# Moving where the low weight halves and the rows of x begin in SBUF, in a one-layer hybrid decoder step

## The chip, the core and the metric

The kernel runs as one program on one core of a Trainium2 chip. The metric is the device time of one execution in microseconds, the median of several runs. The profiled execution is a run of its own: its span is the time from its first to its last recorded instruction, and it has its own device time beside that.

## The reference, cut to what matters

One decoder layer works on 304 tokens: 16 meta tokens, a prompt of 256, and 8 samples of 4 tokens. Nearly all arithmetic is matrix products with float32 weights:

```python
D_MODEL = 2048; D_FF = 5632
def decoder_layer(x, ...):
    xn = rms_norm(x, norm_mix)
    z = xn @ w_in                     # 7456 columns, split between two mixers
    o_a, S_a = rwkv7_mixer(z_a, ...)  # 16 heads of 64, a recurrence over the tokens
    o_b, S_b = retention_mixer(z_b, ...)  # 4 heads of 256, in chunks
    h = x + concatenate([o_a, o_b]) @ w_out
    hn = rms_norm(h, norm_ffn)
    h = h + (silu(hn @ w_gate) * (hn @ w_up)) @ w_down
```

A final norm follows, and the states of both mixers are returned for prompt and samples. The meta tokens are needed by the mixers only: the outputs of the layer have 288 tokens.

## The kernel before, in words

**Tiling.** Features lie on the 128 partitions and tokens run along the free dimension, so a row of x is one feature group `k` (16 of them) with 304 tokens per partition. A weight matrix is cut into blocks of 128 x 128. Four blocks make a tile of 512 columns, which one DMA brings into `wr` in the order of their use.

**Three products for one.** float32 accuracy comes from splitting each operand into two `float32r` halves. ScalarE writes the high half `wh` of a weight tile (a CAST), VectorE the low half `wl = wr - wh`. x is split in the same way into `xh` and `xl`. Each weight block then takes three TensorE matmuls into one accumulator: `wh` with `xh`, `wh` with `xl`, `wl` with `xh` (lines 751 to 753, the three `self.pe.matmul` of `main`). Each has its own weight load, which the profile lists under PEld; it runs beside the matmul before it. All vector, scalar and tensor instructions of the program are listed under line 318, the helper that records them.

**Stages.** First come the 59 blocks of columns of the input projection ("the mixed stages" here), with the mixers' own small matmuls, vector and scalar work between them. The accumulators take 304 columns, 290 (the r columns and two of the loras) or 288 (the retention's q and gates), starting at token 0, 14 or 16 of the row. Then the output projection overwrites the rows `xh` and `xl` with the mixers' outputs, 288 columns of them, and after it with the input of the FFN. The FFN runs gate and up blocks on those rows, and down blocks on activations which lie in the arena `arena_dt.float32r`, also 288 columns.

**Order.** A planner with a cost table decides at build time which step comes next, and the order is then kept on every engine. A first pass (a draft) also measures how long each scratch tile lives; `Room.place` packs them into two arenas, whose limit is `ROOM`.

**Addresses.** Tiles of the pools get SBUF addresses in the order in which the pools were opened (lows, const, weights, scratch) and the tiles made. A row of `xh` is padded from 304 to `XW` = 320 elements, 1280 bytes, so that all rows begin at the same place modulo 256 bytes. `self.xh` is the view for the mixed stages, `self.xf` the one for the stages behind, shifted by `SHIFT_X` elements. The activations of the FFN are shifted by `SHIFT_A` in the same way. These are the begins in the compiled program, in bytes modulo 256:

| what | before | after |
|---|---|---|
| `wl`, all 5 buffers | 128 | 96 |
| `wh`, all 5 buffers; `wr` | 64 | 64 |
| rows of x, mixed stages, 304 columns | 128 | 144 |
| the same from token 14 (290 columns) | 184 | 200 |
| the same from token 16 (288 columns) | 192 | 208 |
| rows of x behind the mixed stages | 208 | 208 |
| FFN activations in the arena | 208 | 208 |
| `sums` (weights of the small sums) | 224 | 224 |

Of the kernel before, what the change touches and what calls it, by code (L numbers as in the profile page):

```python
# [9 lines left out]
F32R = mybir.dt.float32r  # L10
# [5 lines left out]
P = 128  # L16
D = 2048
KT = D // P
# [4 lines left out]
T = META + SEQ + NB * NS  # L23
# [51 lines left out]
NCV = _o  # L75


SHIFT_X = [20] * KT
SHIFT_A = [20] * 11


LASTK = T - P
KEYS = ((0, META, SEQ, 0), (P, P, NP - P, SEQ), (LASTK, 2 * P, T - 2 * P, SEQ + NP - P))
RMW = SEQ + NP - P + T - 2 * P
ROOM = 33008
WIDE = 3792
FREE, GAPS, TRIES = 800.0, (2000.0, 1000.0, 500.0, 200.0, 50.0, 0.0), 12

# [519 lines left out]
class Step:  # L608
# [213 lines left out]
    def start(self):  # L822
        I = self.I
        self.pvt = self.t([P, NPV], "pv", pool=self.cp)
        self.ones = self.t([P, P], "ones", pool=self.cp)
        self.dve.memset(self.ones, 1.0)

        self.omu = self.t([P, 46], "omu", pool=self.cp)
        self.eps = {}
        for c, e in enumerate((RMS_EPS, GN_EPS, 4 * RMS_EPS), 27):  # L830
            self.eps[e] = self.omu[:, c:c + 1]
            self.pool.memset(self.eps[e], e)
        xh, xl = self.xh, self.xl
        warm = self.t([P, 1], "warm")
        self.act.activation(warm, self.ones[:, :1], AF.Tanh)

        gx = self.t([P, KT + KT * T], "xr")
        self.gx = gx[:, :KT]
        xr = self.xr = gx[:, KT:].rearrange("p (k t) -> p k t", t=T)
        x = lambda a, b: self.sp.dma_start(xr[:, a:b], xT(I)[:, a:b, :])  # L840
        self.sp.dma_start(gx[:, :KT + T], I["xT"][:, :KT + T])
        self.load(2)
        x(1, 2)
        self.load(2)
        self.sp.dma_start(self.pvt, I["pv"])
        x(2, 3)
        self.load(2)
        x(3, 4)
        self.load(2)
        for k in range(4, KT, 2):  # L850
            self.load()
            x(k, k + 2)
        self.converted = 0

        pt = self.ps(WARM)
        for _ in range(WARM):
            self.pe.matmul(pt[:, :P], self.ones, self.ones, start=True, stop=True)
# [1074 lines left out]
    def build(self, gam4):  # L1932
        self.gam4 = gam4
        self.shifts = 0
        self.os, self.on, self.gates, self.ht, self.xs_of = [None] * KT, {}, {}, [], {}
        xh = self.t([P, KT, XW], "xh", F32R, pool=self.cp)
        xl = self.t([P, KT, XW], "xl", F32R, pool=self.cp)
        self.xh, self.xl = xh[:, :, :T], xl[:, :, :T]
        self.xf = [(xh[:, k, s:s + TO], xl[:, k, s:s + TO]) for k, s in enumerate(SHIFT_X)]
        self.xs = [(self.xh[:, k, :], self.xl[:, k, :]) for k in range(KT)]  # L1940
        jobs = [self.z_job(i, self.lora_post(i), c0=META - 2 if i else 0) for i in range(3)]
        for h in range(NPAIR):
            jobs += self.pair_jobs(h)
        for h in range(RH):
            jobs += self.ret_jobs(h) + self.gate_jobs(h)
        jobs += self.out_jobs(0) + self.out_jobs(1) + self.ffn_jobs()
        jobs = {j.key: j for j in jobs}
        self.raws, self.halves, self.rests, self.loaded, self.halved = [], [], [], 0, 0
        self.start()
        self.plan.run(self.main(jobs))  # L1950
        self.flush(all=True)
# [5 lines left out]
def xT(I):  # L1957

    return I["xT"][:, KT:].rearrange("p (k t) -> p k t", t=T)
# [19 lines left out]
def body(tc, I, O):  # L1979
# [6 lines left out]
    rooms[F32R].place(WIDE)  # L1986
    rooms[F32].place(ROOM - rooms[F32R].size)
    with ExitStack() as ctx:
# [23 lines left out]
```

## Time and profile before

| | us |
|---|---|
| median of 3 runs (1532.53 to 1534.03) | 1532.96 |
| the profiled execution: device time | 1533.73 |
| its span | 1532.0 |
| PE (matmuls) busy | 1516.4 |
| DVE (VectorE) busy | 1087.0 |
| ACT (ScalarE) busy | 883.7 |

A matmul's record lasts longer than the distance to the next matmul, since they are pipelined. What a matmul costs when TensorE is never idle is therefore read from starts: the length of an unbroken stretch over the number of matmuls in it. The chain of waits lists such stretches with a start, a length and a count. "acc" are the large products of `main`, "mm" the small ones of the mixers.

### The profile page before, as it was taken

What the parts mean: (1) busy time and instruction counts of PE and PEld (TensorE: products, weight loads), DVE (VectorE), ACT (ScalarE), POOL (GpSimd) and SP (SyncE); (2) the same over time, 40 slices, a digit from 0 to 9 for tenths busy, and PEclk for the clock granted to TensorE, in tenths of its full rate; (3) what the DMA queues carried; (4) which work ended last, traced back from release to release, by engine and by line L of the source; (5) the groups of instructions that cost most, each with busy time, mean ns of one, the idle gap of its engine ahead of it and who ended that gap; (6) DMA issues with size and microseconds to landing.
All of it is one profiled execution on the core that took longest, in us unless ns stands there. A gap on an engine that the chain in (4) does not pass through costs nothing.

```text
span 1532.0 us, 31962 instructions
## 1 busy us (share of the span) xinstructions
PE 1516.4 (99%) x11428; PEld 1498.7 (98%) x11428; DVE 1087.0 (71%) x2769; ACT 883.7 (58%) x2109; POOL 32.1 (2%) x165
## 2 busy tenths in 40 slices
PE   8999999999999999999999999999999999999997
PEld 8999999999999989999999999999999999999997
DVE  6989997999999688776656565656565656565656
ACT  6786779878866875577444444444444444444445
POOL 0010010000000000000000000000000000000000
PEclk9999999999999999999999999999999999999999
DMA  7545543544444369756655555555555555555554
GB/s 234 178 138 158 168 144 115 171 151 148 135 138 132 117 241 320 224 177 212 187 158 172 159 169 162 169 162 166 164 164 165 165 163 167 166 163 165 166 166 131
DMA packets 138927, 258.57 MB, mean 169 GB/s; under 512 B 16272, under 2 KB 22928, under 8 KB 138768
## 3 DMA queue, kind: packets, MB, share of 16 engines
q1 hardware_dynamic: 138768, 256.52, 53.6%
q8 instruction: 91, 1.49, 0.4%
q14 instruction: 68, 0.56, 0.1%
HBM read 242.18 MB, written 14.28 MB: 167 GB/s over the span
## 4 chain that ended last, share of the span: by engine, by line
PE 92%; DVE 3%; ACT 2%; DMA 1%; issue 1%; SPq 0%; DVEq 0%; POOL 0%; ACTq 0%
PE acc L318 82%; PE mm L318 10%; DVE arena_dt.float L318 1%; ACT arena_dt.float L318 1%; DMA wr<-big 1%; DVE wl L318 1%; ACT wh L318 0%; ACT xh L318 0%; DMA arena_dt.float<-xT 0%; DVE xl L318 0%; SPq L318 0%; DVE arena_dt.float32r L318 0%; ACT arena_dt.float32r L318 0%; DVEq L2008 0%; POOL arena_dt.float L318 0%
## 5 line engine op out<-in xcount | busy, mean ns | idle before, releaser
L318 PE MATMUL acc<-xh,wh 128*128 128x288 f32 (+2 forms) x2592 | 787.3, 304 | 2.0 <-ACT wh L318 2.0
L318 PE MATMUL acc<-xh,wl 128*128 128x288 f32 (+2 forms) x2592 | 770.3, 297 | 0.6 <-DVE wl L318 0.6
L318 PE MATMUL acc<-xl,wh 128*128 128x288 f32 (+2 forms) x2592 | 764.2, 295 | 0.0
L318 ACT CAST wh<-wr 128x512 fp32r<-128x512 f32 (+1 forms) x827 | 503.5, 616 | 370.1 <-PE acc L318 322.9
L318 DVE TENSOR_TENSOR wl<-wr,wh 128x512 fp32r<-128x512 f32 (+1 forms) x827 | 561.5, 685 | 128.8 <-ACT wh L318 126.4
L318 PEld LDWEIGHTS acc<-xh,wh 128*128 128x128 f32 x2592 | 487.8, 188 | 6.3 <-issue 2.7
L318 PEld LDWEIGHTS acc<-xl,wh 128*128 128x128 f32 x2592 | 487.8, 188 | 3.0 <-issue 1.9
L318 PEld LDWEIGHTS acc<-xh,wl 128*128 128x128 f32 x2592 | 484.3, 187 | 1.7 <-DVE wl L318 1.4
L318 PE MATMUL acc<-arena_dt.float32r,wh 128*128 128x288 f32 x1408 | 281.5, 295 | 0.2 <-DVE arena_dt.float L318 0.2
L318 PEld LDWEIGHTS acc<-arena_dt.float32r,wh 128*128 128x128 f32 x1408 | 226.7, 189 | 0.6 <-DVE arena_dt.float L318 0.4
L318 PE MATMUL acc<-arena_dt.float32r,wl 128*128 128x288 f32 x704 | 208.8, 297 | 0.0
L318 DVE TENSOR_TENSOR arena_dt.float<-acc,arena_dt.float 128x288 f32<-128x288 f32 (+4 forms) x181 | 72.6, 419 | 156.9 <-PE acc L318 156.3
L318 DVE TENSOR_TENSOR arena_dt.float<-arena_dt.float 128x288 f32<-128x288 f32 (+21 forms) x658 | 159.7, 279 | 8.6 <-ACT arena_dt.float L318 6.3
L318 PE MATMUL mm<-arena_dt.float 128*128 128x128 f32 (+7 forms) x1120 | 161.9, 299 | 2.0 <-ACT arena_dt.float L318 1.2
L318 DVE TENSOR_TENSOR arena_dt.float<-arena_dt.float,acc 128x288 f32<-128x288 f32 (+1 forms) x210 | 94.2, 450 | 95.4 <-PE acc L318 93.9
L318 ACT ACTIVATE arena_dt.float<-arena_dt.float 128x288 f32<-128x288 f32 (+7 forms) x229 | 97.1, 432 | 103.1 <-DVE arena_dt.float L318 101.5
L318 PEld LDWEIGHTS mm<-arena_dt.float 128*128 128x128 f32 (+1 forms) x1120 | 138.4, 181 | 8.2 <-ACT arena_dt.float L318 1.9
L318 PEld LDWEIGHTS acc<-arena_dt.float32r,wl 128*128 128x128 f32 x704 | 131.7, 187 | 0.0
L318 ACT COPY arena_dt.float<-mm 64x64 f32<-64x64 f32 (+11 forms) x338 | 94.9, 289 | 45.0 <-PE mm L318 40.8
L318 ACT COPY arena_dt.float<-arena_dt.float 128x8 f32<-128x8 f32 (+8 forms) x267 | 62.5, 283 | 26.6 <-DVE arena_dt.float L318 25.3
L318 ACT CAST arena_dt.float32r<-arena_dt.float 128x288 fp32r<-128x288 f32 (+6 forms) x117 | 49.7, 429 | 40.5 <-DVE arena_dt.float L318 40.1
L318 DVE TENSOR_TENSOR arena_dt.float32r<-arena_dt.float,arena_dt.float32r 128x288 fp32r<-128x288 f32 (+6 forms) x116 | 52.1, 451 | 18.3 <-ACT arena_dt.float32r L318 18.0
(68 smaller groups left out, 571.7 us busy)
## 6 DMA issues: line engine op xcount, KB each, us to landing
wr<-big SPq DMA_DIRECT2D x823, 256.0 KB, 2.7
arena_dt.float<-s0r SPq DMA_DIRECT2D x24, 512.0 KB, 6.4
out_rts<-arena_dt.float SPq DMA_DIRECT2D x16, 512.0 KB, 4.3
arena_dt.float<-s0w SPq DMA_DIRECT2D x16, 256.0 KB, 3.2
arena_dt.float<-xT SPq DMA_DIRECT2D x4, 576.0 KB, 6.3
arena_dt.float<-lora SPq DMA_DIRECT2D x16, 128.0 KB, 2.7
out_rws<-arena_dt.float SPq DMA_DIRECT2D x8, 256.0 KB, 3.4
arena_dt.float<-xT SPq DMA_DIRECT2D x6, 304.0 KB, 5.8
```

The costliest lines, as they stand in the source:

```text
L318: return self._plan.keep(f(*a, **k))
```

## The change

An unused tile `gap` of 56 elements (224 bytes) is made first in the pool of the lows, so that all tiles behind it lie 224 bytes further on; `omu` in the pool of constants grows by 8 elements (32 bytes), so that the tiles behind that one lie 256 bytes further on and begin where they did modulo 256. The view of x for the mixed stages begins 12 elements into the padded row, and the shift behind them grows from 20 to 28. The limit of the arenas is lowered by 64 elements, to pay for the 256 bytes. The arenas come out with the sizes they had, and every engine issues the same instructions in the same order as before.

```diff
-SHIFT_X = [20] * KT
+FIRST = 12
+SHIFT_X = [28] * KT
 SHIFT_A = [20] * 11
...
-ROOM = 33008
+ROOM = 32944
...
-        self.omu = self.t([P, 46], "omu", pool=self.cp)
+        self.omu = self.t([P, 54], "omu", pool=self.cp)
...
+        gap = self.t([P, 56], "gap", F32R, pool=self.lp)
         xh = self.t([P, KT, XW], "xh", F32R, pool=self.cp)
         xl = self.t([P, KT, XW], "xl", F32R, pool=self.cp)
-        self.xh, self.xl = xh[:, :, :T], xl[:, :, :T]
+        self.xh, self.xl = xh[:, :, FIRST:FIRST + T], xl[:, :, FIRST:FIRST + T]
         self.xf = [(xh[:, k, s:s + TO], xl[:, k, s:s + TO]) for k, s in enumerate(SHIFT_X)]
```

## The prediction

> **What bounds the kernel now.** I read the busy shares first, then the waits of PE, then busy time by stretch.
>
> ```profile
> PE 1516.4 (99%) x11428; PEld 1498.7 (98%) x11428; DVE 1087.0 (71%) x2769; ACT 883.7 (58%) x2109; POOL 32.1 (2%) x165
> ```
>
> ```profile
> PE acc L318 <- ACT wh L318: 2.0, 2, 1.7
> PE acc L318 <- DVE wl L318: 0.6, 3, 0.3
> ```
>
> ```profile
> 400.00:500.00 100.00, 100.00 (x783) 99.88 (x782) 94.20 (x397) 69.56 (x206) 6.11 (x30) 1.00 0.43 132
> 730.00:1490.00 760.00, 760.00 (x5703) 760.00 (x5702) 441.42 (x793) 321.16 (x555) 0.00 (x0) 1.00 0.54 166
> ```
>
> In the last two rows the columns are PE, PEld, DVE, ACT and POOL busy, the granted clock, the DMA share and GB/s. PE waits for weight halves for under 3 us in all. In the FFN (730 to 1490) it is busy without a gap at full granted clock, while DVE is busy for 58% and ACT for 42% of the time. In the mixed stages PE has no gap either, but DVE stands at 94%. So the time is a sum of matmul pitches, from one start to the next, and the question is what sets a pitch. The chain of waits (start, length, what, count) gives it:
>
> ```profile
> 607.24 56.48 PE acc L318 x438
> 687.31 5.44 PE acc L318 x42
> 695.31 4.40 PE acc L318 x33
> 702.28 5.06 PE acc L318 x39
> 709.91 4.80 PE acc L318 x36
> 717.28 4.28 PE acc L318 x33
> 722.41 772.22 PE acc L318 x5790
> 1495.16 21.94 PE acc L318 x168
> ```
>
> All of these are 288-column matmuls on data at 208 modulo 256. Yet the first row has 56.48 / 438 = 128.95 ns each, the seventh 772.22 / 5790 = 133.37 ns, and the short ones between them 129.5, 133.3, 129.7, 133.3 and 129.7. Operands, engine and clock are the same, and the pitch has two values. Single starts show that it isn't a mixture:
>
> ```profile
> 645.24 0.29 PE L318 MATMUL acc<-xh,wl 128*128 128x288 f32 x1
> 645.37 0.29 PE L318 MATMUL acc<-xh,wh 128*128 128x288 f32 x1
> 645.50 0.29 PE L318 MATMUL acc<-xl,wh 128*128 128x288 f32 x1
> 645.63 0.29 PE L318 MATMUL acc<-xh,wl 128*128 128x288 f32 x1
> ...
> 845.32 0.30 PE L318 MATMUL acc<-xh,wl 128*128 128x288 f32 x1
> 845.45 0.30 PE L318 MATMUL acc<-xh,wh 128*128 128x288 f32 x1
> 845.58 0.29 PE L318 MATMUL acc<-xl,wh 128*128 128x288 f32 x1
> 845.72 0.30 PE L318 MATMUL acc<-xh,wl 128*128 128x288 f32 x1
> ```
>
> Three matmuls take 0.39 us in the first piece (645.24 to 645.63) and 0.40 us in the second. Each state repeats itself once it is entered; a stop of the stream (the small matmuls between the short stretches) lets it be entered anew. I read this as PE's own reads of SBUF meeting each other: the columns of one matmul are read while the weights of the next are loaded (PEld busy 760.00 of 760.00 us), and where they meet hangs on both addresses and on the phase in which the stream started. DVE and ACT start and stop all through the FFN without breaking the rhythm, so they are not the cause. The FFN fell into the long rhythm at 722.41 and had no stop until 1494.63.
>
> **The change part by part.** *Work.* No instruction is added, removed or moved: all five engines have the same sequence, the arenas the same sizes and places within. `gap` is never written. So every term is a change of duration.
>
> *Writes of VectorE and ScalarE at the new places.* `wl` is now written at 96 and, in the first 40 us, x at 144.
>
> ```profile
> L318 DVE TENSOR_TENSOR wl<-wr,wh 128x512 fp32r<-128x512 f32 x823 | 559.9, 686 | 127.8 <-ACT wh L318 125.4 <-PE acc L318 1.3
> L318 DVE TENSOR_TENSOR xl<-arena_dt.float,xh 128x288 fp32r<-128x288 f32 x16 | 6.8, 453 | 1.9 <-ACT xh L318 1.9
> L318 ACT ACTIVATE xh<-arena_dt.float 128x304 fp32r<-128x304 f32 x16 | 8.3, 544 | 4.0 <-DMA arena_dt.float<-xT 4.0
> L318 ACT ACTIVATE xh<-arena_dt.float,pv 128x288 fp32r<-128x288 f32 x16 | 7.8, 530 | 9.9 <-DVE arena_dt.float L318 9.9
> ```
>
> The second row writes at 208, 16 bytes off a multiple of 64, the first at 128, on it: (686 - 453) / (512 - 288) = 1.04 ns an element, and 288 x 1.04 + 153 = 453, with 686 - 512 x 1.04 = 153, puts both on a plain line through a usual fixed part. ScalarE: 544 - 530 = 14 ns for 16 more elements, on 128 and 208. I take nothing for these writes. The cover is thin in the mixed stages alone: 10 ns more on each of their some 240 `wl` subtractions would be 2.4 us on DVE at 94%, and at most that on the path.
>
> *FFN: `wl` from 128 to 96.* x and activations stay at 208, `wh` at 64, so of the three weight loads one meets other addresses, and the lows begin in the middle of a 64-byte piece. The only row with weights at such a begin is the small sums (`sums`, 224), too short for a rhythm. Bounds: the short rhythm that the same stage has shown, (133.37 - 128.95) x 5790 = **-25.6 us**; a longer one. For the latter I need a step. The rhythms seen are, for three matmuls of 288 columns, 3 x 128.95 = 386.9, 3 x 133.37 = 400.1, and, with x at 192 in the mixed stages, this one:
>
> ```profile
> 390.69 5.51 PE acc L318 x42
> 452.45 12.80 PE acc L318 x96
> ```
>
> 5.51 / 42 = 131.2 ns, 393.6 for three; the other is 133.3 again. The steps are some 6.6 ns a triple, 2.2 ns a matmul. One step longer would be 2.2 x 5790 = +12.7 us, two +25.5 us; I take one as the bound. Of the two sides I take the short rhythm: the pitch of 133.4 is the longest that an unbroken stretch of 288 columns shows here, and two thirds of its meetings keep their places, so a new third has more ways to break it than to lengthen it. But this is a judgment and not a row: of five short stretches with everything at the old places three were short and two long, so that the rhythm may well be drawn at the stop before it.
>
> *Mixed stages: x from 128 to 144, 184 to 200, 192 to 208.* The pitches now:
>
> ```profile
> 126.72 11.17 PE acc L318 x81
> 78.13 2.43 PE acc L318 x18
> L318 PE MATMUL acc<-xh,wh 128*128 128x304 f32 x512 | 161.8, 316 | 0.0
> L318 PE MATMUL acc<-xh,wh 128*128 128x288 f32 x256 | 79.8, 312 | 0.2 <-ACT wh L318 0.2
> L318 PE MATMUL acc<-xh,wh 128*128 128x290 f32 x144 | 44.3, 308 | 0.0
> ```
>
> The first stretch is 304 columns, 137.9 ns; the second mostly 290, 135.0; 288 has 131.2 to 133.3, middle 132.2. The counts of the last three rows are times three: 1536, 768 and 432. At 208 the rows of 288 columns are where the later stages read, so 128.95 to 133.37: -2.5 to +0.9 us. For the others I scale these pitches by columns, an estimate: 304 gets 136.1 to 140.8 (-2.8 to +4.5 us), 290 gets 129.8 to 134.3 (-2.2 to -0.3 us). Sum -7.5 to +5.1 us, and the stream is broken by small matmuls every few microseconds, so both rhythms should occur: I take the middle, **-1 us**.
>
> *Sum.* 1533.7 (the profiled execution) - 25.6 - 1 = 1507.1; that execution is 0.8 above the median of 1532.96, so 1506 to 1507 against the median. DVE and ACT can follow a 3.3% faster FFN (58% and 42% busy), and DMA stands at a share of 0.54.
>
> The Trainium skill ("TensorE: Matmul & The Clock Gate", section "Wait — 56ns, not 53.3ns?") has a rule that speaks against this change: back-to-back warm matmuls start N / 2.4 GHz + about 2.5 ns apart, which makes 122.5 ns for 288 columns (an estimate from that page), and addresses don't enter. By it the edit would be worth nothing and the time stay at 1533; the rows above with 128.95 and 133.37 ns for the same instruction do not agree with it.
>
> **The rivals.**
>
> *Unchanged rhythm.* The FFN falls into a cycle of 133.4 ns again, because the two loads of `wh` set it, or because the entry does. For it: the stretch from 722.41 follows the same small matmuls, at the same place in the order, as it will in the changed kernel. Against: a third of the meetings move. Only the mixed term is left, 1526 to 1539, middle 1532.
>
> *A middle rhythm.* 131.2 ns, as at 390.69: (133.37 - 131.2) x 5790 = -12.6, so 1533.7 - 12.6 - 1 = 1520.
>
> *A longer rhythm, the other side.* A load of `wl` that begins inside a 64-byte piece touches nine of them where it touched eight, and the matmul that runs beside it (`wh` with `xl`, in all triples of the FFN) gives up one step more: +12.7 us, and with it the output projection, now at 128.95, falls to 133.4 (768 matmuls x 4.4 = +3.4 us): 1533.7 + 12.7 + 3.4 - 1 = 1549, or 1546 without the latter. It decides as soon as the FFN's pitch is over 133.6 ns. For it: with the lows at 128 the matmul beside their load is the quickest of the three (starts 845.45, 845.58, 845.72), so that place can lose more than it can gain.
>
> **How the numbers follow.** Short rhythm 0.36; middle 0.14; unchanged 0.27; longer 0.23. A measurement of this kernel can tell 0.2%, 3 us, from no change. Short and middle count as faster, of the unchanged 0.07 is faster, 0.11 within and 0.09 slower: faster 0.57, same 0.11, slower 0.32. The forecast is the likeliest, 1507; its own range is 1501 to 1512 (the mixed term's ends). As the other cases hold most of the rest, the range reaches from 1501 to 1547.
>
> **What would show it right or wrong.** The chain of waits has the verdict: the long stretch from about 720 us with 5790 matmuls should last 747 us (128.95 each); 760 would be the middle rhythm, 772 the unchanged, 785 the longer. The stretch of 438 before it tells whether the output projection kept 56.5 us. Stretches of 304 columns should lie between 136.1 and 140.8 ns. DVE's mean for `wl` should stay at 686 ns; over 700 my line for the writes is wrong. The forecast is wrong if the rhythm is drawn at the last stop, independent of where `wl` lies: then the runs of the changed kernel might not even agree with each other.

## The result and the profile after

The changed kernel takes 1506.74 us, the median of 4 runs (1505.9 to 1507.59), against 1533.0 us before (1532.53 to 1534.03): a ratio of 0.9828, 95% interval 0.9811 to 0.9845. The span of the profiled execution went from 1532.0 to 1504.0 us.

The chain of waits of the changed kernel (start, length, what, count of matmuls), the pieces that answer to those of before:

```profile
126.26 11.18 PE acc L319 x81
389.87 5.43 PE acc L319 x42
451.35 9.57 PE acc L319 x74
543.98 5.54 PE mm L319 x58
604.67 56.48 PE acc L319 x438
684.66 5.43 PE acc L319 x42
692.62 4.27 PE acc L319 x33
699.42 5.04 PE acc L319 x39
706.99 4.66 PE acc L319 x36
714.17 4.27 PE acc L319 x33
719.30 743.59 PE acc L319 x5769
1466.43 22.67 PE acc L319 x168
```

The long stretch now has 743.59 / 5769 = 128.9 ns a matmul. The short stretches ahead of it, which alternated between 129.5 and 133.3 ns, all have 129.2 to 129.4. From the start of the long stretch to that of the last one the FFN takes 1466.43 - 719.30 = 747.13 us, against 1495.16 - 722.41 = 772.75 before: -25.6 us. The stretch of 58 small matmuls at the end of the mixed stages, which stood at 545.02 before, starts 1.0 us earlier, the long stretch 3.1 us earlier. Behind it the last stretch went the other way, from 21.94 to 22.67 us. In sum -25.6 - 3.1 + 0.7 = -28.0 us, the whole difference of the spans. Not all of the 3.1 us is the change's: the section on the prediction takes them apart.

The timeline shows the short rhythm in the FFN, three matmuls in 0.39 us (844.82 to 845.21), and the long one in the last stretch, three in 0.40 us (1474.81 to 1475.21):

```profile
844.82 0.29 PE L319 MATMUL acc<-xh,wh 128*128 128x288 f32 x1
844.95 0.29 PE L319 MATMUL acc<-xl,wh 128*128 128x288 f32 x1
845.08 0.29 PE L319 MATMUL acc<-xh,wl 128*128 128x288 f32 x1
845.21 0.29 PE L319 MATMUL acc<-xh,wh 128*128 128x288 f32 x1
...
1474.81 0.29 PE L319 MATMUL acc<-arena_dt.float32r,wl 128*128 128x288 f32 x1
1474.94 0.43 PE L319 MATMUL acc<-arena_dt.float32r,wh 128*128 128x288 f32 x2
1475.21 0.29 PE L319 MATMUL acc<-arena_dt.float32r,wl 128*128 128x288 f32 x1
```

VectorE's writes cost what they did, 686 ns for a `wl`:

```profile
L319 DVE TENSOR_TENSOR wl<-wr,wh 128x512 fp32r<-128x512 f32 x823 | 557.7, 686 | 120.5 <-ACT wh L319 115.8 <-PE acc L319 1.3
```

### The profile page after: what moved, and what is told of

Its sections match the earlier page's. It is cut to its first block, busy times and chain, and to the rows that moved or that the text cites. A ratio compares the mean times of both kernels' runs of the same rounds, so it can differ in the third digit from the quotient of the medians.

```text
span 1504.0 us, 31962 instructions
## 1 busy us (share of the span) xinstructions
PE 1489.3 (99%) x11428; PEld 1471.3 (98%) x11428; DVE 1084.7 (72%) x2769; ACT 884.5 (59%) x2109; POOL 32.1 (2%) x165
## 4 chain that ended last, share of the span: by engine, by line
PE 95%; DVE 2%; ACT 1%; issue 0%; DMA 0%; SPq 0%; DVEq 0%; POOL 0%; ACTq 0%
PE acc L319 84%; PE mm L319 11%; DVE arena_dt.float L319 1%; ACT arena_dt.float L319 1%; DVE wl L319 0%; DMA arena_dt.float<-xT 0%; SPq L319 0%; DVE xl L319 0%; ACT arena_dt.float32r L319 0%; ACT wh L319 0%; DVEq L2010 0%; ACT xh L319 0%; POOL arena_dt.float L319 0%; DVE arena_dt.float32r L319 0%; ACT shout L319 0%
## 5 line engine op out<-in xcount | busy, mean ns | idle before, releaser
L319 PE MATMUL acc<-xh,wl 128*128 128x288 f32 (+2 forms) x2592 | 762.3, 294 | 0.6 <-DVE wl L319 0.6
L319 PE MATMUL acc<-arena_dt.float32r,wh 128*128 128x288 f32 x1408 | 273.7, 292 | 0.2 <-DVE arena_dt.float L319 0.2
L319 PEld LDWEIGHTS acc<-arena_dt.float32r,wh 128*128 128x128 f32 x1408 | 223.5, 188 | 0.6 <-DVE arena_dt.float L319 0.4
L319 ACT COPY arena_dt.float<-arena_dt.float 128x8 f32<-128x8 f32 (+8 forms) x267 | 62.5, 283 | 27.6 <-DVE arena_dt.float L319 26.3
```

The costliest lines, as they stand in the source:

```text
L319: return self._plan.keep(f(*a, **k))
```

## The experiments

### Which of the two moves it is

One kernel is the changed one, with the lows at 96, and x put back at 128 in the mixed stages:

```diff
-FIRST = 12
+FIRST = 8
```

> The lows at 96 as in the change, x back at 128 in the mixed stages and at 208 behind them. Theory of the lows (their begin at 96 takes the long rhythm away): the long FFN stretch at 128.9 ns a matmul, 1507 to 1511 us. Theory of the draw (both rhythms exist at either place, the last stop before the long stretch draws one): 1507 or 1533, whichever comes. Theory of x (the rows of the mixed stages set the phase in which the FFN is entered): 1533 us, 133.4 ns.

1507.67 us (1506.66 to 1509.32), a ratio to the kernel before of 0.983 (0.9813 to 0.9846). Its long stretch:

```profile
722.78 743.59 PE acc L319 x5769
```

The other starts from the kernel before, leaves the lows at 128, and moves x to 144 in the mixed stages:

```diff
+FIRST = 4
 SHIFT_X = [20] * KT
...
-        self.xh, self.xl = xh[:, :, :T], xl[:, :, :T]
+        self.xh, self.xl = xh[:, :, FIRST:FIRST + T], xl[:, :, FIRST:FIRST + T]
```

> x at 144 in the mixed stages as in the change, the lows back at 128. Theory of the lows: the FFN at 133.4 ns as before, 1529 to 1534 us, with only the mixed term of the change (some 2 us by its profile, whose long output-projection stretch starts at 604.67 instead of 607.24). Theory of the draw: 1507 or 1533. Theory of x: 1507 us, 128.9 ns.

1534.2 us (1533.3 to 1537.23), a ratio of 1.0008 (0.9999 to 1.0018), and the long rhythm:

```profile
723.66 772.22 PE acc L319 x5790
```

So the gain belongs to the lows; the theory of x falls. The place of x in the mixed stages moves nothing that these times can tell, but the traces can. These are the first long stretch of the mixed stages and the 58 small matmuls at their end, in pairs: the kernel before, the change, the lows moved alone, x moved alone:

```profile
27.06 9.82 PE acc L318 x72
545.02 5.55 PE mm L318 x58
26.76 9.82 PE acc L319 x72
543.98 5.54 PE mm L319 x58
28.24 9.87 PE acc L319 x72
546.74 5.53 PE mm L319 x58
28.26 9.91 PE acc L319 x72
547.33 5.53 PE mm L319 x58
```

From start to start that is 518.0 us before and 517.2 with the change, but 518.5 with the lows alone and 519.1 with x alone. The kernels with stops, whose mixed stages are those of before or of the change, agree with these two to 0.1 us. Each move by itself makes the mixed stages longer, and only both together make them shorter; 1.1 us more, and not some 2 us less, is what x alone does there.

Still, one kernel at each place doesn't say whether the lows take the long rhythm away or only drew another one at the last stop.

### Stops, to draw the rhythm many times

Small matmuls of 128 to 143 columns (the trace shows each as two) ahead of every fourth down block stop the stream, so that it starts anew 44 times at phases of its own:

```diff
             acc = accs[key]
+            if k == 0 and key[0] == "down" and key[2] % 4 == 2:
+                self.stops = getattr(self, "stops", 0) + 1
+                self.pe.matmul(self.ps(1)[:, :128 + self.stops % 16], self.ones, self.cst[:, :128 + self.stops % 16], start=True, stop=True)
```

> The kernel before with 44 extra small matmuls of ones, 128 to 143 columns long, ahead of every fourth down block in the FFN: each stops the stream and lets the rhythm be entered anew at another phase; they leave nothing out. A stop costs some 0.2 us, 9 us in all. Both theories: of the 44 stretches between the stops some run at 128.9 and some at 133.4 ns, since the short stretches of before show both; 1518 to 1540 us.

1528.89 us, a ratio of 0.9974 (0.9958 to 0.9989): with 44 matmuls more it is faster than without. Its chain shows why, some stretches in order:

```profile
751.82 0.22 PE mm L318 x2
752.04 6.20 PE acc L318 x48
758.24 0.23 PE mm L318 x2
758.47 55.71 PE acc L318 x432
814.17 0.23 PE mm L318 x2
814.40 6.39 PE acc L318 x48
820.79 0.23 PE mm L318 x2
821.02 6.39 PE acc L318 x48
...
909.51 57.59 PE acc L318 x432
```

55.71 / 432 = 129.0 ns, 57.59 / 432 = 133.3 ns, and the short pieces 129.2 and 133.1. Leaving out the first matmuls behind a stop, of the 44 stretches behind the stops 27 run in the short and 17 in the long rhythm, and none in any other; the stretch ahead of the first stop is long too. (The expectation for the lows at 64 below counts 28 and 17; one of its short ones is too many.) What is drawn depends on the stop: the lengths of the stops repeat after 16, and so do the draws, in all 44 (the stretches of 432 go short, short, long, long, and again).

> The changed kernel with the same 44 stops; they leave nothing out. Theory of the lows: all stretches run at 128.9 ns whatever the phase of the stop, 1507 + 9 = 1516 us at most. Theory of the draw: a mixture as in the kernel before with stops, the share of 133.4 ns about the same, 1518 to 1540 us.

1517.74 us (1516.53 to 1518.95), 1.7 us over what was expected at most. All 44 stretches settle at 128.9 ns, such as:

```profile
756.08 55.70 PE acc L319 x432
831.30 55.70 PE acc L319 x432
```

So with the lows at 96 the draw hardly matters: 44 of 44 against 27 of 44. The long rhythm isn't abolished, though: the changed kernel without stops fell into it in its last stretch, after a wait for VectorE.

### The kernel before with a better draw

The first four of these stops, alone, in the kernel before, with no address moved (the edit is against the kernel with all 44):

```diff
-            if k == 0 and key[0] == "down" and key[2] % 4 == 2:
+            if k == 0 and key[0] == "down" and key[2] % 4 == 2 and key[1] == 0:
```

> The kernel before, no address moved, with the first four of the 44 stops alone; nothing is left out. With all 44, the stretch behind the fourth stop ran at 128.9 ns. Theory of the draw at the last stop: the rhythm now lasts from that stop to the end of the FFN, some 5350 matmuls at 128.9 instead of 133.4 ns, so 1533 - 23 + 1 = 1511 us. If the long rhythm comes back by itself without a stop: more, up to 1534 us.

1508.52 us (1508.32 to 1510.73), a ratio of 0.9844 (0.9828 to 0.9861):

```profile
738.67 6.20 PE acc L318 x48
744.87 0.22 PE mm L318 x2
745.10 6.39 PE acc L318 x48
751.49 0.22 PE mm L318 x2
751.72 6.20 PE acc L318 x48
757.91 0.23 PE mm L318 x2
758.14 708.41 PE acc L318 x5496
```

Short, long, short, and then 708.41 / 5496 = 128.9 ns to the end. Four matmuls of a fifth of a microsecond bring nearly the whole gain at the old addresses: a rhythm, once entered, stays for 700 us.

### What about 96 it is

Two theories: that the lows begin in the middle of a 64-byte piece, or that their distance to the other operands counts. The changed kernel with stops and the lows at 160, 64 or 224; the rest of the gap is moved behind them, so that nothing else shifts (here for 160):

```diff
-        gap = self.t([P, 56], "gap", F32R, pool=self.lp)
+        gap = self.t([P, 8], "gap", F32R, pool=self.lp)
+        gap2 = self.t([P, 48], "gap2", F32R, pool=self.cp)
```

> The changed kernel with the 44 stops, the lows at 160 instead of 96 (the rest of the gap moved behind them, so that x and all else stays); nothing is left out. Theory of the half piece (what counts is that the lows begin 32 bytes into a 64-byte piece): all stretches of the FFN short, 128.9 ns, 1518 us. Theory of the distance (what counts is where the lows lie against x at 208 and the highs at 64, modulo 256): other pitches or a mixture, 1518 to 1540 us or more.

> The same with the lows at 64, where the highs begin too. Theory of the half piece: a mixture as with the lows at 128 (28 short, 17 long stretches there), 1525 to 1532 us. Theory of the distance: anything else.

> The same with the lows at 224. Theory of the half piece: all stretches short, 1518 us. Theory of the distance: a mixture or other pitches.

They took 1536.8, 1529.15 and 1541.44 us in one run each. Stretches of 432 matmuls, first with the lows at 160, then at 64, then at 224:

```profile
760.91 57.12 PE acc L319 x432
837.93 56.32 PE acc L319 x432
```

```profile
759.16 56.17 PE acc L319 x432
835.09 56.64 PE acc L319 x432
```

```profile
763.24 57.13 PE acc L319 x432
840.29 57.13 PE acc L319 x432
```

At 160 these are 132.2 and 130.4 ns (57.12 / 432 and 56.32 / 432; four of the stretches of 48 settle at a third, 131.1), at 64 they are 130.0 and 131.1, and at 224 nearly all is 132.2. Each place of the lows has its own set of rhythms. 160 and 224 begin inside a 64-byte piece as 96 does and have no stretch of 128.9, so the theory of the half piece falls. Places 32 and 192 and 0 were not tried.

If distance is what counts, all places may be moved together. Two kernels do that to the change with stops, by 32 and by 64 bytes (`gap` left out, or cut to 8 elements, and `ROOM` given back):

```diff
-ROOM = 32944
+ROOM = 33000
...
-        gap = self.t([P, 56], "gap", F32R, pool=self.lp)
```

> The changed kernel with the 44 stops and every place 32 bytes further on: lows at 128, highs at 96, x and activations of the later stages at 240, x of the mixed stages at 176. All distances modulo 256 are those of the change; the places within a 64-byte piece are others (lows now on a multiple of 64). Nothing is left out. Theory of the distance: all 44 stretches short, 128.9 ns, 1518 us. If the place within a piece of 64 counts too: other pitches, 1520 to 1545 us.

> The same with every place 64 bytes further on: lows at 160, highs at 128, x behind the mixed stages and activations at 16, x of the mixed stages at 208. Distances and places within a piece of 64 are those of the change. Nothing is left out. Theory of the distance, alone or with the place within a piece: all short, 1518 us. If single places modulo 256 count (lows at 160 gave 130.4 and 132.2 ns with the rest unmoved): those pitches, some 1537 us.

1518.51 and 1517.44 us, one run each, beside 1517.74 for the change with its stops. All 45 stretches of both, the 44 and the one ahead of the first stop, settle at 128.9 ns; the first two of 432 in the kernel moved by 32:

```profile
758.07 55.70 PE acc L319 x432
833.30 55.70 PE acc L319 x432
```

With the lows at 128, as in the kernel before, but x at 240 and the highs at 96, the long rhythm does not come. And with the lows at 160 and all the rest moved along, the pitches of 130.4 and 132.2 are gone. No single place counts here, and not the place within 64 bytes; the distances do: the lows 112 and the highs 144 bytes below x. Only what is left of them modulo 256 bytes can count: the rows of x lie 1280 bytes apart, and all of them run at one pitch. Whether the lows have to lie right against x or against the highs is not shown: moving the lows alone changed both distances.

### The same distance for the 304 columns

If distance alone set the pitch, the 304 columns of the mixed stages would do best at 208 too. The changed kernel with a second gap ahead of x (and `omu` and `ROOM` to match):

```diff
-SHIFT_X = [28] * KT
+SHIFT_X = [12] * KT
...
+        gap2 = self.t([P, 16], "gap2", F32R, pool=self.cp)
```

> The changed kernel without stops, x of the mixed stages at 208 instead of 144 (its 290 columns from 8, its 288 from 16); lows, highs and all behind the mixed stages as in the change. Nothing is left out. Theory of the distance: the 304 columns now lie against the weights as the FFN's rows do and take the short rhythm of that place, 128.9 x 304 / 288 = 136.1 ns at most against 138.5 (1536 of them: -3.7 us), while the 768 of 288 columns leave their good place and may go back from 129.6 to 131 to 132 (+1.1 to +1.8 us): 1503 to 1506 us, against 1507 of the change.

1509.04 us (1508.62 to 1509.95), a ratio of 0.9838 (0.9825 to 0.9852) to the kernel before: outside what was expected, and not better than the change. The chain has, for 304 columns and for 288:

```profile
127.91 11.34 PE acc L319 x81
392.63 5.58 PE acc L319 x42
```

11.34 / 81 = 140.0 ns against 138.0 with x at 144, and 5.58 / 42 = 132.9 against 129.3. The 288 columns lost their good place as expected. The 304 columns did not take up the short rhythm at the distance where 288 do, 136.1 ns if it grew with the columns: how long the row is counts beside the distance. So 144 is a good choice for the mixed stages as far as tried, and no version here beats the change.

## Why the prediction was right

**What bounds the kernel.** Right: but for some 2 us of starts and waits (below), nothing changed on the path but the pitch of the large matmuls. PE waits as little as before, and DVE and ACT, busy for as long as before, followed the quicker FFN.

**Two rhythms with the same operands.** Right, and now more than read from a trace: stops alone turn one into the other at unmoved addresses. That PE's own reads meet is still argued, not shown; what is shown is that VectorE's and ScalarE's work can be left alone while addresses or stops change the pitch.

**The FFN term.** -25.6 us predicted, -25.6 measured. But the ground for choosing this side, that a moved third "has more ways to break it than to lengthen it", was weak: of four places of the lows tried at these places of x and of the highs (128, 160, 64, 224), none but the old one has any stretch of 128.9 ns, and the shortest rhythm elsewhere is 130.0. 96 is a good place by its distances, not because places in general are better than 128. The size was well founded, since 288 columns at the same places had shown the short rhythm; that the side came out was in part luck.

**The mixed term.** -1 us predicted, and -1.0 measured at the end of the mixed stages; 0.3 us of it is the earlier start of the first stretch (26.76 against 27.06), so that -0.7 us are left. Its parts, from the starts of all matmuls there: 288 columns went from 131.7 to 129.6 ns (768 of them, -1.6 us, inside the bounds), 304 stayed at 138.4 to 138.5, and 290 went from 134.1 to 134.5 (+0.2 us). For 290 the bounds by scaled columns (129.8 to 134.3) were just missed, and the 140.0 ns of 304 columns at 208 show that the short rhythm doesn't scale. The term was luck besides: it counted the move of x alone, and x alone costs 1.1 us there. That the lows move against x in these stages too was put at nothing, and it is what turns the sign.

**The writes.** `wl` stayed at 686 ns, as forecast, but the line that the forecast went by shows nothing: two unknowns were fitted to two rows, so any two rows would lie on it.

**What the sum lacked.** The 0.3 us at the start, another 2.1 us between 545 and 720 us, and the last stretch, which drew the long rhythm, +0.7 us. Of the 2.1 us, 0.5 lie behind 607 us, where stretches of 33 and 36 matmuls turned short. The other 1.5 lie ahead of the output projection and are not the addresses' work: from the 58 small matmuls to that stretch it took 62.2 us before and 60.7 with the change, but 61.1 at the old addresses with four stops and 62.4 with all places 64 bytes further on. In the kernel before, PE waited twice there (0.57 and 0.26 us, for VectorE and ScalarE), and the chain of waits goes back to a weight transfer of 9.00 us. Together the span is 28.0 us shorter where the sum had 26.6; the medians, which hold less of such chance, are 26.3 us apart.

**The rivals.** *Unchanged*: its mechanism, a rhythm drawn at the entry, is real in the kernel before, where four stops are worth 24 us; with the lows at 96 none of the 44 draws went the other way, and only the last stretch of the change did. *Middle*: pitches of 131.1 exist, with the lows at 64. *Longer*: no place tried had a rhythm of 288 columns over 133.3 ns, and its mechanism, nine pieces of 64 bytes instead of eight, falls: with all places moved by 32 bytes the lows touch eight again, and the pitch stays at 128.9, while with the lows at 64 they touch eight and have 130.0 or 131.1.

**The rule of the Trainium skill** in "TensorE: Matmul & The Clock Gate" ("Wait — 56ns, not 53.3ns?"), N / 2.4 GHz + about 2.5 ns, gives 122.5 ns for 288 columns (an estimate from that page). No stretch came below 128.9 ns, and the six pitches between that and 133.3 do not agree with a rule without addresses for these float32r streams.

## What to carry to other kernels

When TensorE is busy without a gap, compare the pitch of equal matmuls between stretches (length over count in the chain of waits): two values for the same instruction mean a rhythm that was entered at the last stop, and the time of a long stream can hang on that one draw. Insert some cheap stops of different lengths to see which rhythms a layout has before judging it by one run, and move operands by their distances modulo 256 bytes until all draws give the short one. Try each row length by itself, because a distance that is good for one was bad for the other.

## What the runs showed that was not expected

Steady pitches for 288 columns were 128.9, 130.0, 130.4, 131.1, 132.2 and 133.3 ns, so the steps are between 0.4 and 1.1 ns, finer than the 2.2 ns that the prediction took. A kernel with 44 useless matmuls was faster than the same without them (0.9974), since most of its draws were better than the one it had had. And the pitch did not care where operands lie by themselves: the same distances gave 128.9 ns at three places 32 bytes apart.
